# A decoder step's S5 seam: output gates and branch splits reordered, S5 output tiles computed in pairs

## The chip, the cores and the metric

One Trainium2 chip; the kernel runs on 1 of its cores. The metric is device microseconds (us) of one execution. Engines of the core, as the profile names them: PE (TensorE matmul), PEld (TensorE weight load, which overlaps PE), DVE (VectorE), ACT (ScalarE), POOL (GpSimd) and SP (SyncE, which here only issues DMAs).

## The reference, cut to what matters

One layer for 512 prompt tokens and 32 sample tokens (544 columns in all), model width 1024. An S5 branch (a diagonal state-space scan) and an HGRN2 branch (a gated linear recurrence) run side by side on one input projection and are merged by sigmoid gates; an MLP follows.

```python
h = rms_norm(x, norm_mix_pre)
proj = h @ w_in + b_in
u, q, f, i, g, gate_s5, gate_hg = jnp.split(proj, SPLIT_POINTS, axis=-1)
y_s5 = s5_mixer(u, ...)          # scan, gelu, then y * sigmoid(y @ w_glu + b_glu)
y_hg = hgrn2_mixer(q, f, i, g, ...)  # recurrence, norm, then o * silu(g)
merged = sigmoid(gate_s5) * (y_s5 @ w_br_s5) + sigmoid(gate_hg) * (y_hg @ w_br_hg)
x = x + rms_norm(merged @ w_out, norm_mix_post)
```

Further outputs are the new states of both branches.

## The kernel before, in words

**Products.** Every large product is computed in fp32r with operands split into a high part (`wh`, `xh`) and a low part (`wl`, `xl`): three matmuls per 128 x 128 block of weights, each for two halves of the 544 columns, so six matmuls per block (`dense`, L108 to L116). ACT casts the high part of a weight block (`S.copy(wh, wt)`, L99), DVE subtracts for the low part (L71). The same two-step cut of an activation is `split` (ACT L132, then DVE L71). `weights` (L83) loads one block by SP into one of 3 `wt` buffers and cuts it into one of 2 `wh` and 2 `wl` buffers. An output tile of `dense` lies in PSUM, in one of 2 `psd` buffers.

**Order of work.** The program's planner places each engine's instructions one after the other: among those that it holds ready, the one traced earliest goes first. `tc.high_priority(offset=n)` makes an instruction count as traced n instructions earlier; `WAHEAD` is 100 (weights), `EAHEAD` 50 (reading out a PSUM tile). `tc.manual_schedule(engines=...)` keeps the listed engines in the order written. The whole middle of the kernel (L1038 to L1063) is written by hand for PE alone.

**Fill queue.** In that middle, PE's small matmuls of the recurrences are interleaved with steps of the large products. A queue `fill.todo` holds generators, one per output tile; each step (`next`) is one block of 128 rows, six matmuls, and a tile has 8 steps. `fill.run(n)` takes n steps at a place in the code; the constants F1, F2, F3, FH, FY, FD (L480) are those n. The queue holds tiles of the HGRN2 inputs, then pairs of `hgrn_gate` tiles (silu(g), multiplied into `yhg`: ACT L522, DVE L74, DVE L71) and sigmoid gate tiles (`gate_tiles`, ACT L1016): 2 and 3, eight gate tiles, 4 and 5, eight gate tiles, 6 and 7; and last the eight `br_hg` tiles (yhg @ w_br_hg). When `s5_tables` starts, four steps of one of the first eight gate tiles, three more of them, and all behind them are left. `hgrn_gate` 6 and 7 are appended (L1057) after all gate tiles.

**S5 in the middle.** `s5_tables` (L834) computes tables on DVE (`ct`, `st`; `QR`, `QN` on SBUF of `Er`, `Ei`) and stores them to DRAM. `s5_late` (L922) runs for two halves of the groups, hf = 0 and 1: load `U`, `PT`, `Q`, `tab`; matmuls `psdS`; a scan on DVE; FH = 22 fill steps; `HB` from the scan (ACT L977); matmuls `psy` in four parts with FY = 3 steps between; FD = 12 steps after hf = 0; then the result goes to DRAM (`y_d`). `PT` and `HB` share memory, so `PT` and `U` of hf = 1 load after the last `psy` of hf = 0.

**HGRN2 branch.** The first step of `br_hg(0)` traces the cuts of its input (`split(*ys_[k], yhg[:, k])`, L1029). The tiles `yh`, `yl` use the memory of `hh`, `hl`, the projection's input, so a cut can run only when the last projection tile has read its block k.

**S5 output.** After the middle (L1069 on): `yt` comes back from DRAM, is cut to `zh`, `zl`; four tiles `ps_gl` (y @ w_glu), each followed by two sigmoids (L1093, L1095), the product `yn` on DVE and the cut to `sh`, `sl`; then eight tiles `ps_bs` (y_s5 @ w_br_s5), each followed by a product with the gate (which frees the PSUM buffer), a sum and a cut (`ms_`). Four weight blocks hold two tiles each. Here no engine's order is written by hand.

Of the kernel before, what the change touches and what calls it, by code (L numbers as in the profile page):

```python
# [9 lines left out]
F32 = mybir.dt.float32  # L10
# [35 lines left out]
def layer(ctx, tc, a, o):  # L46
# [23 lines left out]
    def tt(out, x, y, op, e=None):  # L70
        (e or V).tensor_tensor(out=out, in0=x, in1=y, op=op)  # L71
# [13 lines left out]
    def weights(src, name, res=None, ahead=WAHEAD):  # L85

        n = 1
        for d in src.shape[1:]:
            n *= d
        if len(src.shape) == 3:  # L90
            src = src.rearrange("p a b -> p (a b)")
        elif len(src.shape) == 4:
            src = src.rearrange("p a b c -> p (a b c)")
        with tc.high_priority(offset=ahead):
            wt = wp.tile([P, n], F32, tag="wt", name=f"wt_{name}", bufs=3)
            nc.sync.dma_start(out=wt, in_=src)
# [11 lines left out]
    def dense(ps, wh, wl, xs, first=True, last=True):  # L108

        n = len(xs)  # L110
        for k, (xh, xl) in enumerate(xs):
            c = slice(k * P, (k + 1) * P)
            f, l = first and k == 0, last and k == n - 1
            for w, x, st, sp in ((wh, xh, f, False), (wh, xl, False, False), (wl, xh, False, l)):
                for i in range(2):
                    mm(ps[:, i, 0:int(np.prod(x[i].shape[1:]))], lhsT=w[:, c], rhs=x[i], start=st, stop=sp)  # L116
# [11 lines left out]
    def dense_tile(name):  # L128
        return psd.tile([P, 2, 512], F32, tag="d", name=name)

    def split(hi, lo, src):
        S.copy(hi, src)  # L132
        tt(lo, src, hi.bitcast(F32), SUB)
# [343 lines left out]

    fill = Fill()

    F1, F2, F3, FL, FK, FO, FN, FH, FY, FD, FS = 44, 1, 32, 5, 4, 2, 3, 22, 3, 12, 2  # L480


    def hgrn_in(g, gp):
# [33 lines left out]
    def hgrn_gate(h, gp):  # L517
        m = 28 + h
        ps = yield from inproj(m)
        sg = gp.tile([P, 2, HT], F32, tag="sg", name=f"sg{m}")  # L520
        with tc.high_priority(offset=EAHEAD):
            S.activation(sg, ps[:, :, 0:HT], AF.Sigmoid, bias=b_in[:, m:m + 1])  # L522
            stt(sg, ps[:, :, 0:HT], b_in[:, m:m + 1], sg, ADD, MUL)
        y = yhg[:, h].rearrange("p (a b) -> p a b", a=2)
        tt(y, y, sg, MUL)
# [499 lines left out]
    def br_hg(m):  # L1025
        if m == 0:
            ys_ = pair_k("y")
            for k in range(8):
                split(*ys_[k], yhg[:, k])  # L1029
            yx.extend(views(ys_))  # L1030
        wh, wl = weights(a["w_br_hg"][m], f"bh{m}")
        ps = dense_tile(f"ps_bh{m}")
        yield from dense_steps(ps, wh, wl, yx)
        with tc.high_priority(offset=EAHEAD):
            gv = sgate[1][m].rearrange("p (a b) -> p a b", a=2)
            tt(gv, ps[:, :, 0:HT], gv, MUL)

    with tc.manual_schedule(engines={ET.PE}):  # L1038
        T = [hgrn_in(g, gp) for g in range(3)]
        s5a = ExitStack()  # L1040
        s5k = s5_parameters(s5a.enter_context(tc.tile_pool(name="s5a", bufs=1, reuse_waits="tile", side="right")))
        with tc.tile_pool(name="hcore", bufs=1, reuse_waits="tile", side="right") as hp:
            scT = [hp.tile([P, 2, NP_], F32, tag=f"scT{i}", name=f"scT{i}") for i in range(2)]
            scS = [hp.tile([NS, 2, NS], F32, tag=f"scS{i}", name=f"scS{i}") for i in range(2)]
            qm = hp.tile([P, 2, 8 * 36], F32, tag="qm", name="qm")
            for t in scT + scS + [qm]:
                G.memset(t, 0.0)
            for g in range(4):
                if g:
                    fill.add(hgrn_gate(2 * g - 2, gp), hgrn_gate(2 * g - 1, gp))  # L1050
                if g == 1:
                    T.append(hgrn_in(3, gp))
                elif g:
                    sgate[3 - g] = gate_tiles(3 - g)
                hgrn_core(g, T[g], hp, scT, scS, qm)
        s5a.close()
        fill.add(hgrn_gate(6, gp), hgrn_gate(7, gp))  # L1057
        with tc.tile_pool(name="s5p", bufs=1, reuse_waits="tile", side="right") as sp:
            s5_tables(sp, s5k)
        fill.add(*(br_hg(m) for m in range(8)))  # L1060
        fill.run(F3)
        with tc.tile_pool(name="s5", bufs=1, reuse_waits="tile") as sp:
            s5_late(sp, s5k)  # L1063
        fill.run()
# [4 lines left out]
    with tc.tile_pool(name="glu", bufs=1, reuse_waits="tile") as lp:  # L1069
        yt = lp.tile([P, 4, 576], F32, tag="yt", name="yt")  # L1070
        for k in range(4):
            nc.gpsimd.dma_start(out=yt[:, k].rearrange("p (t x) -> p t x", t=8),
                                in_=y_d.rearrange("t c g x -> c g t x")[4 * k:4 * k + 4]
                                .rearrange("c g t x -> (c g) t x"))
        zh = lp.tile([P, 4, 576], F32R, tag="zh", name="zh")
        zl = lp.tile([P, 4, 576], F32R, tag="zl", name="zl")
        for k in range(4):
            split(zh[:, k], zl[:, k], yt[:, k])
        sv = lambda z: [z[:, 0:288], z[:, 288:576].rearrange("p (t x) -> p t x", t=4)[:, :, 0:64]]
        zx = [(sv(zh[:, k]), sv(zl[:, k])) for k in range(4)]  # L1080
        b_glu = lp.tile([P, 4], F32, tag="b_glu", name="b_glu")
        nc.gpsimd.dma_start(out=b_glu, in_=a["b_glu"])
        sh = lp.tile([P, 4, NT], F32R, tag="sh", name="sh")
        sl = lp.tile([P, 4, NT], F32R, tag="sl", name="sl")
        for mc in range(2):
            wh, wl = weights(a["w_glu"][mc], f"gl{mc}")
            for i in range(2):
                m = 2 * mc + i
                ps = dense_tile(f"ps_gl{m}")
                dense(ps, wh[:, 512 * i:512 * i + 512], wl[:, 512 * i:512 * i + 512], zx)  # L1090
                with tc.high_priority(offset=EAHEAD):
                    sg = lp.tile([P, 8, 72], F32, tag="sgl", name=f"sgl{m}", bufs=2)
                    S.activation(sg[:, 0:4].rearrange("p t x -> p (t x)"), ps[:, 0, 0:288], AF.Sigmoid,  # L1093
                                 bias=b_glu[:, m:m + 1])
                    S.activation(sg[:, 4:8, 0:64], ps[:, 1, 0:256].rearrange("p (t x) -> p t x", t=4), AF.Sigmoid,  # L1095
                                 bias=b_glu[:, m:m + 1])
                    yn = lp.tile([P, 2, HT], F32, tag="yn", name=f"yn{m}", bufs=2)
                    yv = yt[:, m].rearrange("p (t x) -> p t x", t=8)
                    pv = lambda z: z[:, :, 0:64].rearrange("p t (h j) -> p h j t", h=2)
                    sv2 = lambda z: z[:, 0:4, 64:72].rearrange("p t (h j) -> p h j t", h=2)  # L1100
                    tt(yn[:, :, 0:256].rearrange("p h (j t) -> p h j t", t=8), pv(yv), pv(sg), MUL)
                    tt(yn[:, :, 256:HT].rearrange("p h (j t) -> p h j t", t=4), sv2(yv), sv2(sg), MUL)
                    split(sh[:, m], sl[:, m], yn.rearrange("p a b -> p (a b)"))
        sx = [(halves(sh[:, k]), halves(sl[:, k])) for k in range(4)]
        if "dbg_ys5" in o:
            nc.sync.dma_start(out=o["dbg_ys5"], in_=sh.bitcast(F32))
        for mc in range(4):
            wh, wl = weights(a["w_br_s5"][mc], f"bs{mc}")
            for i in range(2):
                m = 2 * mc + i  # L1110
                ps = dense_tile(f"ps_bs{m}")
                dense(ps, wh[:, 512 * i:512 * i + 512], wl[:, 512 * i:512 * i + 512], sx)
                with tc.high_priority(offset=EAHEAD):
                    gt = sgate[0][m]
                    gv = gt.rearrange("p (a b) -> p a b", a=2)
                    tt(gv, ps[:, :, 0:HT], gv, MUL)
                    tt(gt, gt, sgate[1][m], ADD)
                    split(*ms_[m], gt)
    hin.close()
    kept.close()  # L1120
    S.activation(scr1, ms_[7][0][:, 0:1], AF.Abs_reciprocal_sqrt, scale=0.0, bias=one_t)
# [597 lines left out]
```

## Time and profile before

| | us |
|---|---|
| three executions | 965.05, 965.63, 968.43 (median 965.63) |
| the profiled execution | 966.16 |
| its span, first to last instruction | 964.3 |
| PE busy | 943.5 (98%) |
| PEld busy | 919.8 (95%) |
| DVE busy | 621.8 (64%) |
| ACT busy | 446.2 (46%) |

All times in rows are from the start of the span. A row of a timeline gives start, duration, engine, line, operation, tiles, and in brackets how long the engine was idle before it and what ended that. Matmuls are pipelined: one that takes 0.29 us by its row is followed by the next after 0.127 us.

### The profile page before, as it was taken

To read this page: it belongs to the slowest core of one execution; us is meant where nothing else is said; L and a number is where in the kernel's file an instruction comes from. 1 tells how busy PE (TensorE), PEld (TensorE's weight loads), DVE (VectorE), ACT (ScalarE), POOL (GpSimd) and SP (SyncE) were. 2 spreads that over 40 slices of the span, in tenths; PEclk is the share of its full clock that TensorE was granted. 3 is DMA by queue.
4 is the path that set the end of the run, shared out by engine and by line. 5 is a ranking of instruction groups with operands and counts; after the bars stand their busy time and mean duration, and the time that the engine had idled before them with its cause. 6 is when DMAs were issued, how large, how long until landed. Compare 5 with 4: busy or idle time off the path is not lost.

```text
span 964.3 us, 21356 instructions
## 1 busy us (share of the span) xinstructions
PE 943.5 (98%) x9124; PEld 919.8 (95%) x9124; DVE 621.8 (64%) x1158; ACT 446.2 (46%) x835; POOL 62.6 (6%) x104
## 2 busy tenths in 40 slices
PE   8999999999999999999999999999999999999995
PEld 5999999989999999999999999999999999999994
DVE  6777669486693888558368558463673475447747
ACT  5744364544534523564243647343562265216623
POOL 2100000000000000422100000000100110010000
PEclk9999999999999999999999999999999999999998
DMA  7352242142423437666432514334544454356502
GB/s 251 98 147 67 67 135 71 50 155 67 149 68 91 140 125 249 223 193 205 131 91 88 175 45 158 110 109 122 133 151 102 107 155 131 103 125 167 180 2 92
DMA packets 45407, 121.26 MB, mean 126 GB/s; under 512 B 9121, under 2 KB 12577, under 8 KB 44673
## 3 DMA queue, kind: packets, MB, share of 16 engines
q1 hardware_dynamic: 37664, 97.20, 31.5%
q0 software_dynamic: 7360, 22.15, 8.8%
q8 instruction: 71, 1.16, 0.5%
q10 hardware_dynamic: 288, 0.56, 0.2%
q14 instruction: 24, 0.19, 0.1%
HBM read 101.66 MB, written 17.06 MB: 123 GB/s over the span
## 4 chain that ended last, share of the span: by engine, by line
PE 87%; DVE 6%; ACT 3%; DMA 2%; issue 2%; SPq 0%; DVEq 0%; ACTq 0%; POOLq 0%
PE ps_in L116 23%; PE ps_d L116 17%; PE ps_u L1324 8%; PE ps_u L126 7%; PE ps_bh L116 5%; PE ps_uy L1324 4%; PE ps_o L116 3%; PE ps_e L126 2%; PE ps_o L126 2%; PE ps_bs L116 2%; PE psL L643 2%; PE ps_uz L1324 2%; PE ps_u L116 1%; DMA tab<-tab_d 1%; PE psO L709 1%
## 5 line engine op out<-in xcount | busy, mean ns | idle before, releaser
L116 PE MATMUL ps_in<-hh,wh_in 128*128 128x272 f32 x736 | 159.0, 297 | 0.0
L116 PE MATMUL ps_in<-hl,wh_in 128*128 128x272 f32 x736 | 153.0, 289 | 0.0
L116 PE MATMUL ps_in<-hh,wl_in 128*128 128x272 f32 x736 | 152.3, 288 | 0.0
L116 PEld LDWEIGHTS ps_in<-hh,wh_in 128*128 128x128 f32 x736 | 115.3, 189 | 3.1 <-issue 1.8
L116 PEld LDWEIGHTS ps_in<-hl,wh_in 128*128 128x128 f32 x736 | 115.7, 189 | 0.0
L116 PEld LDWEIGHTS ps_in<-hh,wl_in 128*128 128x128 f32 x736 | 115.7, 188 | 0.0
L71 DVE TENSOR_TENSOR wl_in<-wt_in,wh_in 128x1024 fp32r<-128x1024 f32 (+1 forms) x54 | 61.7, 1144 | 61.1 <-ACT wh_in L99 58.5
L116 PE MATMUL ps_d<-a0l,wh_d 128*128 128x272 f32 x448 | 93.5, 290 | 0.0
L116 PE MATMUL ps_d<-a0h,wl_d 128*128 128x272 f32 x448 | 93.5, 290 | 0.0
L116 PE MATMUL ps_d<-a0h,wh_d 128*128 128x272 f32 x448 | 92.9, 289 | 0.4 <-DVE ov L71 0.4
L99 ACT CAST wh_in<-wt_in 128x1024 fp32r<-128x1024 f32 x46 | 48.3, 1052 | 91.3 <-PE ps_in L116 90.7
L116 PEld LDWEIGHTS ps_d<-a0h,wh_d 128*128 128x128 f32 x448 | 70.7, 188 | 0.6 <-PE ps_d L116 0.6
L116 PEld LDWEIGHTS ps_d<-a0h,wl_d 128*128 128x128 f32 x448 | 70.3, 188 | 0.9 <-DVE wl_d L71 0.6
L116 PEld LDWEIGHTS ps_d<-a0l,wh_d 128*128 128x128 f32 x448 | 70.6, 189 | 0.0
L71 DVE TENSOR_TENSOR ov<-ps_d,ov 128x544 f32<-128x544 f32 x24 | 17.4, 724 | 61.7 <-PE ps_d L116 61.7
L71 DVE TENSOR_TENSOR wl_d<-wt_d,wh_d 128x1024 fp32r<-128x1024 f32 x28 | 34.2, 1220 | 24.4 <-ACT wh_d L1277 18.9
L1277 ACT CAST wh_d<-wt_d 128x1024 fp32r<-128x1024 f32 x26 | 27.0, 1047 | 29.5 <-PE ps_d L116 18.1
L71 DVE TENSOR_TENSOR wl_S<-wt_S,wh_S 128x1024 fp32r<-128x1024 f32 x24 | 29.3, 1219 | 11.4 <-ACT wh_S L1277 11.4
L1277 ACT CAST wh_S<-wt_S 128x1024 fp32r<-128x1024 f32 x24 | 25.2, 1050 | 10.1 <-PE ps_d L116 10.1
L676 DVE COPY_PREDICATED scT<-masks,psL 32x128 f32<-32x128 uint8 x80 | 28.3, 354 | 2.3 <-PE psS L646 0.2
L116 PE MATMUL ps_bh<-yl,wh_bh 128*128 128x272 f32 x128 | 26.8, 291 | 1.4 <-DVE yl L71 1.4
L116 PE MATMUL ps_bh<-yh,wh_bh 128*128 128x272 f32 x128 | 27.1, 293 | 0.0
(552 smaller groups left out, 2312.5 us busy)
## 6 DMA issues: line engine op xcount, KB each, us to landing
wt_in<-in_w_in SPq DMA_DIRECT2D x52, 512.0 KB, 3.8
wt_d<-in_w_down SPq DMA_DIRECT2D x28, 512.0 KB, 3.9
wt_A<-in_w_up SPq DMA_DIRECT2D x12, 512.0 KB, 4.1
wt_S<-in_w_up SPq DMA_DIRECT2D x24, 256.0 KB, 2.7
wt_S<-in_w_up POOLq DMA_DIRECT2D x24, 256.0 KB, 4.6
s<-in_hg_s SPq DMA_DIRECT2D x8, 512.0 KB, 4.4
out_hg_s<-s SPq DMA_DIRECT2D x8, 512.0 KB, 3.6
wt_bh<-in_w_br_hg SPq DMA_DIRECT2D x8, 512.0 KB, 3.9
```

The lines of the kernel that those rows point to most:

```text
L71: (e or V).tensor_tensor(out=out, in0=x, in1=y, op=op)
L99: S.copy(wh, wt)
L116: mm(ps[:, i, 0:int(np.prod(x[i].shape[1:]))], lhsT=w[:, c], rhs=x[i], start=st, stop=sp)
L126: mm(ps[:, i, 0:HT], lhsT=ws[i][j][:, c], rhs=x[hf], start=st, stop=sp)
L643: mm(pq[sq * y:sq * y + m, 4 * i + w], lhsT=k[:, i, c:c + m], rhs=up(c, c + sq, i), start=True, stop=True)
L676: V.copy_predicated(blocks(sc[r], h)[:, :, y, :, 1], masks[r, L].rearrange("p x (n h) -> p x n h", h=h), pq[r].rearrange("p x (n h) -> p x ...
L709: mm(po[:, w], lhsT=sc[:, i, c], rhs=vt[:, i, w], start=True, stop=(w == 0))
L1277: S.copy(h, t)
L1324: mm(ps, lhsT=w[:, c], rhs=x_[:, k], start=(first and k == 0 and j == 0), stop=(k == 3 and j == 2), skip_group_check=True)
```

## The change

Five edits. FD goes from 12 to 9. The cuts of the HGRN2 branch's input are traced as if 400 instructions earlier. `hgrn_gate` 6 and 7 are put behind the tile in progress at the head of the fill queue, not at its end. ACT's order in the S5 output is written by hand: both `w_glu` blocks first, then the outputs of `ps_gl` 0 and 1, the first block of `w_br_s5`, the outputs of 2 and 3, the second block; in the `ps_bs` part the block after next comes ahead of the outputs of a pair. And `ps_bs` tiles 0 and 1 are computed together: blocks 0 to 2 of both, then block 3 of both; the outputs of every pair follow its two tiles.

```diff
-    F1, F2, F3, FL, FK, FO, FN, FH, FY, FD, FS = 44, 1, 32, 5, 4, 2, 3, 22, 3, 12, 2
+    F1, F2, F3, FL, FK, FO, FN, FH, FY, FD, FS = 44, 1, 32, 5, 4, 2, 3, 22, 3, 9, 2
@@ br_hg
-            for k in range(8):
-                split(*ys_[k], yhg[:, k])
+            with tc.high_priority(offset=400):
+                for k in range(8):
+                    split(*ys_[k], yhg[:, k])
@@ after the last hgrn_core
-        fill.add(hgrn_gate(6, gp), hgrn_gate(7, gp))
+        fill.todo[1:1] = [hgrn_gate(6, gp), hgrn_gate(7, gp)]
@@ S5 output; gl_out(m, ps) and bs_out(m, ps) hold the outputs' code as it was
-        for mc in range(2):
-            wh, wl = weights(a["w_glu"][mc], f"gl{mc}")
-            for i in range(2):
-                m = 2 * mc + i
-                ps = dense_tile(f"ps_gl{m}")
-                dense(ps, wh[:, 512 * i:512 * i + 512], wl[:, 512 * i:512 * i + 512], zx)
...
-        for mc in range(4):
-            wh, wl = weights(a["w_br_s5"][mc], f"bs{mc}")
-            for i in range(2):
-                m = 2 * mc + i
-                ps = dense_tile(f"ps_bs{m}")
-                dense(ps, wh[:, 512 * i:512 * i + 512], wl[:, 512 * i:512 * i + 512], sx)
...
+        wb = {}
+        with tc.manual_schedule(engines={ET.Activation}):
+            wg = [weights(a["w_glu"][mc], f"gl{mc}") for mc in range(2)]
+            for m in range(4):
+                c = slice(512 * (m % 2), 512 * (m % 2) + 512)
+                ps = dense_tile(f"ps_gl{m}")
+                dense(ps, wg[m // 2][0][:, c], wg[m // 2][1][:, c], zx)
+                gl_out(m, ps)
+                if m == 1:
+                    wb[0] = weights(a["w_br_s5"][0], "bs0")
+            wb[1] = weights(a["w_br_s5"][1], "bs1")
+            for mc in range(4):
+                wh, wl = wb[mc]
+                ps = [dense_tile(f"ps_bs{2 * mc + i}") for i in range(2)]
+                for ks in ((range(3), (3,)) if mc == 0 else (range(4),)):
+                    for i in range(2):
+                        for k in ks:
+                            c = slice(512 * i + k * P, 512 * i + k * P + P)
+                            dense(ps[i], wh[:, c], wl[:, c], sx[k:k + 1], first=(k == 0), last=(k == 3))
+                if mc < 2:
+                    wb[mc + 2] = weights(a["w_br_s5"][mc + 2], f"bs{mc + 2}")
+                for i in range(2):
+                    bs_out(2 * mc + i, ps[i])
```

## Rows read from the trace of the kernel before

**Rows 1.** PE's waits from 350 to 560: who, for whom, us, times, longest.

```profile
PE ps_bh L116 <- DVE yl L71: 1.4, 1, 1.4
PE ps_bs L116 <- ACT sh L132: 0.9, 1, 0.9
PE psy L990 <- ACT HB L977: 0.5, 1, 0.5
PE ps_bs L116 <- ACT sgl L1095: 0.2, 1, 0.2
```

**Rows 2.** Busy time by stretch: the stretch, its length, each engine, clock, DMA share, GB/s.

```profile
core 0: us, PE busy (x) PEld busy (x) DVE busy (x) ACT busy (x) POOL busy (x), PEclk, DMA share, GB/s
350.00:550.00 200.00, 197.08 (x1701) 195.18 (x1700) 133.85 (x205) 90.84 (x139) 29.45 (x44) 1.00 0.52 168
```

**Rows 3.** Chain of waits, a stretch of unbroken product: start, us, what.

```profile
468.06 22.84 PE ps_bh L116 x180
```

**Rows 4.** Timeline of PE, 429.8 to 436.9, where `br_hg` begins.

```profile
430.17 0.51 PE L116 MATMUL ps_bh<-yh,wh_bh 128*128 128x272 f32 x2
...
432.07 0.52 PE L116 MATMUL ps_bh<-yl,wh_bh 128*128 128x272 f32 x2 [1.39 <-DVE yl L71]
...
434.27 2.44 PE L949 MATMUL psdS<-U,PT 128*64 128x80 f32 x64
```

**Rows 5.** Timeline of ACT, 423 to 437.

```profile
423.86 3.82 ACT L980 COPY Tg<-T 128x2048 f32<-128x2048 f32 x1
...
428.20 1.04 ACT L99 CAST wh_bh<-wt_bh 128x1024 fp32r<-128x1024 f32 x1
429.14 0.44 ACT L1000 ACTIVATE gsq<-gsq 128x288 f32<-128x288 f32 x1
429.48 3.37 ACT L132 CAST yh<-yhg 128x544 fp32r<-128x544 f32 x6
```

**Rows 6.** Tile U, 420 to 436: its load's issue, and the load's time to landing.

```profile
L930 POOL DMA_DIRECT2D U<-u_d x1: 537/537/537, 424.1 to 424.1; - x1
...
DMA to landing us min/median/max: 6.2/6.2/6.2
```

**Rows 7.** Timeline of DVE, 345 to 386, in `s5_tables`.

```profile
349.39 0.78 DVE L74 SCALAR_TENSOR_TENSOR sg<-ps_in,b_in,sg 128x544 f32<-128x544 f32 x1
...
350.82 0.71 DVE L71 TENSOR_TENSOR yhg<-yhg,sg 128x544 f32<-128x544 f32 x1
...
366.62 1.23 DVE L71 TENSOR_TENSOR wl_in<-wt_in,wh_in 128x1024 fp32r<-128x1024 f32 x1 [3.25 <-ACT wh_in L99]
...
382.41 1.23 DVE L71 TENSOR_TENSOR QN<-QN,t 128x1024 f32<-128x1024 f32 x1
```

**Rows 8.** Timeline of ACT, 364 to 412, through hf = 0 of `s5_late`.

```profile
366.49 0.72 ACT L1016 ACTIVATE gate_q<-ps_in,b_in 128x544 f32<-128x544 f32 x1
...
390.74 0.62 ACT L940 COPY rh<-ex 128x512 f32<-128x512 f32 x1 [6.16 <-DMA q_d<-QN]
...
403.99 3.82 ACT L980 COPY Tg<-T 128x2048 f32<-128x2048 f32 x1
...
407.82 1.23 ACT L977 COPY HB<-di 64x504 f32<-64x504 f32 x2
```

**Rows 9.** Timeline of PE, 407.9 to 409.8.

```profile
409.19 0.48 PE L990 MATMUL psy<-HB,Q 128*128 128x144 f32 x2 [0.48 <-ACT HB L977]
```

**Rows 10.** Tile ps_bs: matmuls, ns min/median/max, first and last start.

```profile
L116 PE MATMUL ps_bs<-sh,wh_bs x64: 286/288/393, 502.8 to 527.9; 128*128 128x272 f32 x64
```

**Rows 11.** Timeline of ACT, 490 to 516.

```profile
503.60 1.04 ACT L99 CAST wh_bs<-wt_bs 128x1024 fp32r<-128x1024 f32 x1
504.55 0.50 ACT L1093 ACTIVATE sgl<-ps_gl,b_glu 128x288 f32<-128x288 f32 x1
```

**Rows 12.** Timeline of DVE, 500 to 520.

```profile
501.67 1.34 DVE L71 TENSOR_TENSOR yn<-yt,sgl 128x32 f32<-128x32 f32 x2
...
504.68 1.23 DVE L71 TENSOR_TENSOR wl_bs<-wt_bs,wh_bs 128x1024 fp32r<-128x1024 f32 x1 [0.23 <-ACT wh_bs L99]
...
509.42 0.72 DVE L71 TENSOR_TENSOR gate_q<-ps_bs,gate_q 128x544 f32<-128x544 f32 x1 [0.86 <-PE ps_bs L116]
```

More of the change, by code (lines that the diff above doesn't have):

```diff
@@ L1084, in layer @@
         sl = lp.tile([P, 4, NT], F32R, tag="sl", name="sl")
-        for mc in range(2):
-            wh, wl = weights(a["w_glu"][mc], f"gl{mc}")
-            for i in range(2):
-                m = 2 * mc + i
-                ps = dense_tile(f"ps_gl{m}")
-                dense(ps, wh[:, 512 * i:512 * i + 512], wl[:, 512 * i:512 * i + 512], zx)
[L1091 to L1103, printed above, removed]
@@ new lines, in gl_out @@
+        def gl_out(m, ps):
+            with tc.high_priority(offset=EAHEAD):
+                sg = lp.tile([P, 8, 72], F32, tag="sgl", name=f"sgl{m}", bufs=2)
+                S.activation(sg[:, 0:4].rearrange("p t x -> p (t x)"), ps[:, 0, 0:288], AF.Sigmoid,
+                             bias=b_glu[:, m:m + 1])
+                S.activation(sg[:, 4:8, 0:64], ps[:, 1, 0:256].rearrange("p (t x) -> p t x", t=4), AF.Sigmoid,
+                             bias=b_glu[:, m:m + 1])
+                yn = lp.tile([P, 2, HT], F32, tag="yn", name=f"yn{m}", bufs=2)
+                yv = yt[:, m].rearrange("p (t x) -> p t x", t=8)
+                pv = lambda z: z[:, :, 0:64].rearrange("p t (h j) -> p h j t", h=2)
+                sv2 = lambda z: z[:, 0:4, 64:72].rearrange("p t (h j) -> p h j t", h=2)
+                tt(yn[:, :, 0:256].rearrange("p h (j t) -> p h j t", t=8), pv(yv), pv(sg), MUL)
+                tt(yn[:, :, 256:HT].rearrange("p h (j t) -> p h j t", t=4), sv2(yv), sv2(sg), MUL)
+                split(sh[:, m], sl[:, m], yn.rearrange("p a b -> p (a b)"))
@@ L1106, in layer, with bs_out @@
             nc.sync.dma_start(out=o["dbg_ys5"], in_=sh.bitcast(F32))
-        for mc in range(4):
-            wh, wl = weights(a["w_br_s5"][mc], f"bs{mc}")
-            for i in range(2):
-                m = 2 * mc + i
-                ps = dense_tile(f"ps_bs{m}")
-                dense(ps, wh[:, 512 * i:512 * i + 512], wl[:, 512 * i:512 * i + 512], sx)
[L1113 to L1118, printed above, removed]
+        def bs_out(m, ps):
+            with tc.high_priority(offset=EAHEAD):
+                gt = sgate[0][m]
+                gv = gt.rearrange("p (a b) -> p a b", a=2)
+                tt(gv, ps[:, :, 0:HT], gv, MUL)
+                tt(gt, gt, sgate[1][m], ADD)
+                split(*ms_[m], gt)
+        wb = {}
[21 more added lines that the diff above has]
+                    bs_out(2 * mc + i, ps[i])
     hin.close()
```

## The prediction

> **What bounds the kernel now.** First PE's list of waits over the stretch that the edits touch, 350 to 560: it has only four entries, and they are the whole room there is [rows 1]. The stretch's busy times say the same: of 200 us PE idles 2.92 between 350 and 550 at full clock [rows 2]. An idle entry understates the loss, since a matmul's row outlasts its successor's start: 180 matmuls took 22.84 us, 0.127 us each [rows 3], so after the two at 430.17 the next was due at 430.42 and came at 432.07, a loss of 1.65 where the row shows 1.39 idle [rows 4]. I add this 0.26 to every entry: the start of `br_hg` 1.65; `psy` of hf = 0 waiting for `HB` 0.74; `ps_bs` waiting for a PSUM buffer that a sigmoid reads 0.45, and for `sh` 1.12. Together 3.96 us, 0.41% of the time. As PE is the path, each number below is time on it, or it is hidden.
>
> The Trainium skill (Trainium Kernel Development and Optimization, Best Practices) would have the distance judged by how busy the weight loads are, not the matmuls. Their row leaves 4.82 us idle in the stretch where the matmuls' leaves 2.92 [rows 2]; by that rule the ceiling of a gain is 4.8 and not 4.0.
>
> **Part 1: what fills PE around the `br_hg` seam (FD, gates, cuts).** The number of steps is the same, so PE's own work is. After `psy` of hf = 0, the queue before has nine projection steps left and then three of `br_hg(0)`; these three start at 430.17 and stall. With FD = 9 the `psdS` matmuls of hf = 1 come exactly at 430.17, and `br_hg(0)` behind them. The 1.65 goes. What is late next:
>
> (a) `psdS` needs `U`, which loads after `psy`: issued at 424.1, landing 6.2 us later, at 430.3 [rows 6]. PE is there at 430.2, and with the restart loses some 0.25. FD takes away the cover of three steps (2.3 us) that this load had; a load 1 us later costs 1 us more.
>
> (b) `psdS` lasts 2.4 (row start 434.27, 64 matmuls, 2.44) [rows 4], so `br_hg(0)` is due at about 432.9. Cuts now outrank weight casts (400 against 100). They can't run early: `yh` lies in `hh`'s memory, block 0 of which the last projection tile, eight steps of 0.76 that end at 430.17, first gives up at 424.9. At that time ACT is in the copy of `Tg`, 423.86 to 427.68 [rows 5]. Before, it took the weights' cast first (428.20) and the cuts after it (429.48, six in 3.37, 0.56 each) [rows 5]. Now the cuts come first as far as they are ready. Seven of them (3.9), one gate output (0.72, [rows 8]), the sigmoid (0.44) and the cast itself (1.04) end at 427.7 + 6.1 = 433.8: PE waits 0.9, and half a microsecond of matmuls later another 0.7 for DVE's low half (1.23 by the like operation of [rows 12]). That is 1.6. Lower end 0, if the cast keeps its place. Upper end 2.9, if the eighth cut and the second gate output (0.56 + 0.72) go ahead as well. I take 1.6, since the new order is just what the offsets say and the rows give every duration of it. If the cast is early instead, the cuts' low halves hold DVE and the scan of hf = 1, whose `HB` now falls due three steps earlier, is the next thing late; I put that inside the same ends.
>
> Seam: -1.65 + 0.25 + 1.6 = +0.2 (ends -1.4 and +1.5).
>
> (c) The gates moved up. Each costs ACT 0.72 and DVE 0.78 + 0.71 [rows 7, 8]. They leave DVE at the seam, where PE no longer waits for them. But gates 4 and 5 are pushed back by two tiles: from 349 on DVE [rows 7] to the tile whose output ACT takes at 366.49 [rows 8] and the one after it. There DVE works on the `QR`/`QN` products, which end at 382.41 + 1.23 = 383.64 [rows 7]. All that follows hangs on that end: the store of `QN`, for which ACT waits until 390.74 (6.16 idle), then the scan, then the copies to `HB` at 407.82 [rows 8], for which PE waits at 409.19 [rows 9]. This chain has no slack; it is 0.74 late already. So DVE work put into it counts in full: 0 at the lower end (hidden in the hole of 3.25 before 366.62 [rows 7]; the new work comes after that hole, so only a rearrangement would do it), 2 x 1.49 = 3.0 at the upper. The first gate's product (0.78) is traced within 50 instructions of the chain and outranks it; the other three operations rank behind it and run only where the chain pauses. At 350.82 such a second product did slip into the table chain [rows 7], which speaks for more. I take +0.8. Gates 6 and 7 add the same 3.0 about 16 steps after the tables begin, well ahead of the hole of 3.25 at 366.62 [rows 7], which takes it up; without it they would cost 3.0 by the same chain.
>
> **Part 2: the S5 output.** PE enters `ps_bs` at 502.8 [rows 10]. Before, ACT cast weights at 503.60 (1.04) ahead of the fourth sigmoid pair at 504.55 [rows 11]. By hand the cast follows, so the sigmoids can start 0.5 to 1.0 earlier: the first `w_br_s5` cast now comes after the outputs of `ps_gl` 1 and pushes tile 2's by up to 1.04, which takes back half; I take 0.5. That frees the PSUM buffer before PE asks for it (505.1): -0.45. With blocks 0 to 2 of both tiles first, 36 matmuls last until 502.8 + 4.6 = 507.4, and `sh` of the fourth tile is then due half a microsecond later than before and comes half a microsecond earlier: -1.12. If one of the two fails, its 0.45 or 1.12 stays.
>
> What it adds: tiles 0 and 1 now end six matmuls apart, at 508.2 and 508.9, and tile 2 needs tile 0's buffer at once. DVE has the product that frees it (0.72 [rows 12]) and the low half of the second block (1.23 [rows 12]), both due in the same microsecond: cast of that block after the last `sh`, low half until about 509.1, product until 509.8, PE waits 0.9 + 0.26, say 1.1. Lower end 0.1 (the product alone), upper 2.5, if the first block's low half, now cast after `ps_gl` 1, also lies behind a `yn` pair (1.34, [rows 12]). ACT's waits in its new order hold only cuts of `ms_`, and those are read after the last `ps_bs` tile, which begins its last block at 527.9 [rows 10]. SP issues the same loads in the same order, into the same three buffers.
>
> Seam: -1.57 + 1.1 = -0.45 (ends -1.5 and +0.9).
>
> **Sum.** +0.2 + 0.8 - 0.45 = +0.55 us. The profiled execution took 966.16 (span 964.3 and 1.86 around it); it would be 966.7. The median shown is 0.53 lower, 965.63: forecast 966.2 us, no change that can be measured. What a measurement of this kernel tells from none is about 0.5%, 4.8 us; the three runs alone lie 3.4 apart.
>
> **Rivals.**
>
> *All four waits go.* The cast keeps its place, the chain of `QN` gets shorter by what left it, the S5 output is clean: -3.96 + 0.25 + 0.1 = -3.6, 962.0. For it: every wait has an edit aimed at it or near it. Against: ACT has 3.8 of `Tg` and some 4.5 of cuts in the 9 us before `br_hg`, and no edit touches the `QN` chain but to add to it.
>
> *Slower: the whole DVE work of gates 4 and 5 lands in the `QN` chain.* Place: DVE, 367 to 384; price 3.0 at `psy` of hf = 0, in place of my 0.8; it decides from the first tenth of a microsecond by which `QN` ends after 383.64. 965.63 + 0.2 - 0.45 + 3.0 = 968.4. For it: the precedent at 350.82. Against: ACT idles 6.16 before 390.74 for the store alone [rows 8], and work that now interrupts the scan behind it could move into that wait.
>
> *The offset does nothing*, because memory and `Tg` hold the cuts anyway and PE waits as long at the new place as at the old: the S5 output alone counts, 965.2.
>
> *A gain up to the weight loads' ceiling*, 4.8: 960.8. Nothing in PE's own list of waits supports the further 0.9.
>
> **How the numbers follow.** Forecast 0.43, its own range 964.5 to 967.5; slower through `QN` 0.29; all waits gone 0.20; offset idle 0.05; weight-load ceiling 0.03. The range takes in both sides: 962.0 at the bottom (the second of these), at the top the upper ends of `br_hg` and `QN` together with the S5 term, 965.63 + 1.5 + 3.0 - 0.45 = 969.7. Faster by over 0.5% means below 960.8, more than all waits hold: 0.03. Slower by over 0.5% means over 970.5, all upper ends at once (+5.4): 0.06. Within: 0.91.
>
> **What would show it.** In PE's waits after: no entry at `ps_bh` for `yl`; a short one at `psdS` for `U`; one at `ps_bh` for `wh_bh` (step b; if it is absent and ACT's cast precedes the cuts, b was wrong). The last `QN` on DVE later than 383.6, and the entry of `psy` for `HB` longer than 0.5 by as much (c). In the S5 output no entry for `sh` or the sigmoid, and one at `ps_bs` for the gate's product on DVE. The prediction fails if PE's idle between 350 and 560 falls below 1.5 us or rises over 6.

## The result, and the profile after

The changed kernel takes 971.53 us (median of 10 runs, 969.30 to 974.14), the kernel before in the same comparison 965.94 (10 runs, 965.05 to 969.93): ratio 1.0052, 95% interval 1.0041 to 1.0064. It is slower, by 5.6 us. Forecast were 966.2 and a range of 962.0 to 969.7.

The profiled execution of the changed kernel took 974.14 us (span 972.3), 8.0 more than the profiled one of before. It is the slowest of the ten executions and shows the lowest mean granted clock of them (0.991; the other nine 0.992 to 0.996), so stretches are read from it with care. To see where the time went, PE's timeline is cut at five first starts: the last `psN` (before anything that was edited), `psFq` (the end of the stretch in which DVE computes the S5 tables), `psy` of hf = 0, `ps_gl`, `ps_o`. The stretch from `psy` to `ps_gl` is called the seam below; the wait for `HB` of hf = 0 lies in it, since the first matmuls of `psy` read parts of `HB` that are ready earlier.

| us | psN to psFq | to psy | to ps_gl | to ps_o | after |
|---|---|---|---|---|---|
| before | 34.18 | 54.77 | 82.42 | 37.83 | 435.70 |
| changed | 39.74 | 55.67 | 84.06 | 36.99 | 435.69 |
| difference | +5.56 | +0.90 | +1.64 | -0.84 | 0 |

The missing 0.76 lies ahead of the last `psN` (319.36 and 320.12); in twelve other profiles that start lies anywhere from 318.5 to 322.4, so it belongs to no edit.

PE's waits in the changed kernel, 320 to 560 (who, for whom, us, times, longest), are the answer to [rows 1]:

```profile
PE ps_in L116 <- DVE t L71: 2.5, 1, 2.5
PE ps_in L116 <- DVE wl_in L71: 1.1, 1, 1.1
PE ps_bh L116 <- ACT wh_bh L99: 0.8, 1, 0.8
PE ps_in L116 <- DVE sg L74: 0.7, 1, 0.7
PE psdS L949 <- DVE ysb L71: 0.6, 1, 0.6
PE ps_bh L116 <- DVE wl_bh L71: 0.5, 1, 0.5
PE ps_bs L116 <- DVE gate_q L71: 0.3, 1, 0.3
PE psdS L949 <- DMA U<-u_d: 0.2, 1, 0.2
```

All four waits of before are gone; eight others stand there. The largest two lie in 325 to 346, where the kernel before had none. From 350 to 560, the stretch that the prediction called the whole room, PE idles 3.13 us after and idled 2.92 before, so the sign written down for failure (over 6) did not show: the loss lies ahead of that window. The row after:

```profile
350.00:560.00 210.00, 206.87 (x1765) 204.97 (x1764) 133.65 (x201) 92.99 (x142) 29.42 (x44) 0.99 0.49 164
```

The busy row of the kernel before for 325 to 345, which I had not read (columns as in [rows 2]):

```profile
325.00:345.00 20.00, 20.00 (x160) 20.00 (x160) 19.96 (x45) 6.61 (x10) 1.60 (x4) 1.00 0.43 125
```

DVE is busy for 19.96 of 20 us there, and PE for all of them. The same row after:

```profile
325.00:345.00 20.00, 16.71 (x130) 16.27 (x129) 20.00 (x45) 6.59 (x10) 1.60 (x4) 1.00 0.34 99
```

DVE's timeline of the changed kernel in that stretch shows what the two gates did to its queue:

```profile
330.53 0.78 DVE L74 SCALAR_TENSOR_TENSOR sg<-ps_in,b_in,sg 128x544 f32<-128x544 f32 x1
...
335.68 1.22 DVE L71 TENSOR_TENSOR wl_in<-wt_in,wh_in 128x1024 fp32r<-128x1024 f32 x1
336.81 1.22 DVE L71 TENSOR_TENSOR t<-Ei,a2i 128x1024 f32<-128x1024 f32 x1
...
341.70 1.22 DVE L71 TENSOR_TENSOR wl_in<-wt_in,wh_in 128x1024 fp32r<-128x1024 f32 x1
...
344.37 0.78 DVE L74 SCALAR_TENSOR_TENSOR sg<-ps_in,b_in,sg 128x544 f32<-128x544 f32 x1
```

and ACT's shows when their inputs were there:

```profile
329.95 1.04 ACT L99 CAST wh_in<-wt_in 128x1024 fp32r<-128x1024 f32 x1
335.16 1.05 ACT L99 CAST wh_in<-wt_in 128x1024 fp32r<-128x1024 f32 x1 [4.17 <-PE ps_in L116]
336.11 0.71 ACT L522 ACTIVATE sg<-ps_in,b_in 128x544 f32<-128x544 f32 x1
```

The cast at 329.95 ends at 331.0, its low half starts 4.7 later, at 335.68; the cast at 335.16 ends at 336.2, its low half starts 5.5 later, at 341.70. The second gate's sigmoid ends at 336.8, and the product that reads the same PSUM tile, and so frees it, starts 7.5 later, at 344.37. In the kernel before DVE's queue had the low half of the cast that ended at 335.45 at once:

```profile
335.48 1.23 DVE L71 TENSOR_TENSOR wl_in<-wt_in,wh_in 128x1024 fp32r<-128x1024 f32 x1
```

So a full DVE does not by itself delay the low halves: before, it was as full, and they came at once. What changed is their place in its queue. Behind the first gate's product (330.53, 0.78), DVE does nothing but table operations from 331.22 to 335.68, and the low half comes after them.

What stood at this place before were sigmoid tiles, which ACT alone reads out of PSUM; a `hgrn_gate` tile hands its buffer to DVE. PE's timeline has both ends of it:

```profile
336.96 0.52 PE L116 MATMUL ps_in<-hh,wl_in 128*128 128x272 f32 x2 [1.08 <-DVE wl_in L71]
...
345.30 0.49 PE L116 MATMUL ps_in<-hh,wh_in 128*128 128x272 f32 x2 [2.52 <-DVE t L71]
...
346.91 0.65 PE L116 MATMUL ps_in<-hh,wh_in 128*128 128x272 f32 x2
```

Start to start the two waits cost 1.23 and 2.68 over the usual 0.127. The low half that was 5.5 late ended at 342.92, while PE stood waiting for the buffer, so it added no wait of its own. The releaser of the second is named `t`, since it ended last; the product at 344.37, which ends just before PE starts, is the one that reads the buffer. And from 346.9 to 350.1 the matmuls start 0.227 apart: 15 times 0.1 is 1.5, nearly all that remains of 5.56. The granted clock of 340 to 350 is 0.84, so part of it ran at the lower level, 1.2 GHz:

```profile
340.00:350.00 10.00, 7.48 (x49) 7.29 (x48) 10.00 (x26) 1.66 (x2) 0.00 (x0) 0.84 0.25 74
```

At the seam, ACT's timeline answers to [rows 5]; the cast of `wh_bh` now comes after all eight cuts:

```profile
430.47 3.82 ACT L980 COPY Tg<-T 128x2048 f32<-128x2048 f32 x1
434.20 1.74 ACT L132 CAST yh<-yhg 128x544 fp32r<-128x544 f32 x3
435.84 0.71 ACT L1016 ACTIVATE gate_v<-ps_in,b_in 128x544 f32<-128x544 f32 x1
436.45 1.73 ACT L132 CAST yh<-yhg 128x544 fp32r<-128x544 f32 x3
438.08 0.44 ACT L1000 ACTIVATE gsq<-gsq 128x288 f32<-128x288 f32 x1
438.43 1.18 ACT L132 CAST yh<-yhg 128x544 fp32r<-128x544 f32 x2
439.51 0.71 ACT L1016 ACTIVATE gate_v<-ps_in,b_in 128x544 f32<-128x544 f32 x1
440.12 1.03 ACT L99 CAST wh_bh<-wt_bh 128x1024 fp32r<-128x1024 f32 x1
```

and PE's answers to [rows 4]:

```profile
437.10 1.88 PE L949 MATMUL psdS<-U,PT 128*64 128x80 f32 x48 [0.19 <-DMA U<-u_d]
439.63 0.78 PE L949 MATMUL psdS<-U,PT 128*64 128x80 f32 x16 [0.65 <-DVE ysb L71]
441.21 0.52 PE L116 MATMUL ps_bh<-yh,wh_bh 128*128 128x272 f32 x2 [0.80 <-ACT wh_bh L99]
...
442.46 0.82 PE L116 MATMUL ps_bh<-yh,wl_bh 128*128 128x272 f32 x2 [0.49 <-DVE wl_bh L71]
```

### The profile page after: what moved, and what is told of

The parts are those of the page before. It is cut to its first block, busy times and chain, and to the rows that moved or that the text cites. A ratio compares the mean times of both kernels' runs of the same rounds, so it can differ in the third digit from the quotient of the medians.

```text
span 972.3 us, 21361 instructions
## 1 busy us (share of the span) xinstructions
PE 947.6 (97%) x9124; PEld 923.8 (95%) x9124; DVE 621.2 (64%) x1158; ACT 445.9 (46%) x835; POOL 62.5 (6%) x104
## 4 chain that ended last, share of the span: by engine, by line
PE 89%; DVE 6%; ACT 3%; issue 1%; DMA 1%; SPq 0%; DVEq 0%; ACTq 0%
PE ps_in L116 24%; PE ps_d L116 17%; PE ps_u L1344 7%; PE ps_u L126 7%; PE ps_bh L116 5%; PE ps_uy L1344 4%; PE ps_o L116 2%; PE ps_bs L116 2%; PE ps_e L126 2%; PE ps_o L126 2%; PE psL L643 2%; PE ps_uz L1344 2%; PE ps_gl L116 1%; PE ps_u L116 1%; DVE t L71 1%
## 5 line engine op out<-in xcount | busy, mean ns | idle before, releaser
L116 PE MATMUL ps_bh<-yh,wl_bh 128*128 128x272 f32 x128 | 27.4, 296 | 0.5 <-DVE wl_bh L71 0.5
```

## The experiments

Theory A, after the result: gates 6 and 7 are the loss, because they put DVE work into the stretch where DVE has no free time. Rivals: the PSUM buffer, held until DVE reads it, and not DVE's time; the place in PE's own order; FD = 9 and the offset, not the gates. Each kernel is compared with the kernel before in its own runs on the same chip (median 966.71, 968.33 and 966.35 in the three groups of four), so ratios are what to compare. All compute the whole layer.

**One part undone, one part alone**

`e1_gates_last`, the changed kernel with the gates at the end of the queue again:

```diff
-        fill.todo[1:1] = [hgrn_gate(6, gp), hgrn_gate(7, gp)]
+        fill.add(hgrn_gate(6, gp), hgrn_gate(7, gp))
```

> The changed kernel with hgrn_gate 6 and 7 back at the end of the fill queue, all else as changed. Theory A: the loss is the two gate tiles run while DVE computes the S5 tables: in the profile after, PE waits there for wl_in (1.1 idle) and for sg (2.5 idle), runs some 15 matmuls at 0.227 us instead of 0.127 behind it, and waits 0.7 more for the next gate pair; 5.6 + 1.0 us in all by the same points of both timelines. Then this one takes 965 to 967 us (ratio to before 0.999 to 1.001). Rival B: the loss is at the br_hg seam (offset 400 and FD = 9), where the profile after shows 0.2, 0.6, 0.8 and 0.5 idle: then it stays at 970 or more (ratio over 1.004).

968.33 us, ratio 1.0015 (1.0002 to 1.0027). The tables' stretch is back at 34.18 to the hundredth. The rest is 84.86 from `psy` to `ps_gl` (2.44 more than before) and -0.86 in the S5 output. The ratio lies above the range of A (up to 1.001) and below that of B (from 1.004): some two thirds of the loss are the gates' place, and what is left is the seam.

`e2_gates_alone`, the kernel before with that line alone:

```diff
-        fill.add(hgrn_gate(6, gp), hgrn_gate(7, gp))
+        fill.todo[1:1] = [hgrn_gate(6, gp), hgrn_gate(7, gp)]
```

> The kernel before with only hgrn_gate 6 and 7 moved up. Theory A: it carries the whole loss, 5 to 7 us, less what the br_hg seam wins back when the gates have left it (at most 1.7): 969 to 972 us (ratio 1.003 to 1.007), with the wait for sg at ps_in near 342. Rival B: 965 to 966.5.

970.91, ratio 1.0041 (1.0026 to 1.0055). Tables 38.24, with the same two waits, 1.1 and 2.5; the stretch to `psy` +0.77; the seam 82.13, 0.3 better than before (its wait for `yl` shrinks from 1.4 to 0.9, and the one for `HB` grows from 0.5 to 0.9). One edit of a line makes most of the loss. Here the matmuls behind the 2.5 stay 0.127 apart, and the row of 340 to 350 has the clock at 1.00 beside the same busy time of PE as above:

```profile
340.00:350.00 10.00, 7.48 (x60) 7.29 (x59) 10.00 (x24) 1.66 (x2) 0.00 (x0) 1.00 0.26 76
```

`e3_s5out_alone`, the kernel before with the S5 output of the changed one (both functions, ACT's order by hand, tiles 0 and 1 together); against the changed one:

```diff
-    ... = 44, 1, 32, 5, 4, 2, 3, 22, 3, 9, 2
+    ... = 44, 1, 32, 5, 4, 2, 3, 22, 3, 12, 2
-            with tc.high_priority(offset=400):
-        fill.todo[1:1] = [hgrn_gate(6, gp), hgrn_gate(7, gp)]
+        fill.add(hgrn_gate(6, gp), hgrn_gate(7, gp))
```

> The kernel before with only the S5 output as changed (ACT's order by hand, tiles in pairs). From the two profiles the stretch from ps_gl to ps_o became 0.85 us shorter: waits of 0.2 and 0.9 idle gone, one of 0.3 for the gate's product new. Theory A and rival B both say 964.8 to 965.4 (ratio 0.999); the prediction's term of -0.45 says 965.5.

965.97, ratio 0.9990 (0.9979 to 1.0001). The S5 output is 36.99 in place of 37.83, with one wait left, 0.3 for `gate_q`. It does what it says; 0.84 of 966 is at the edge of what these runs can tell. The stretches ahead, which this kernel does not edit, are 55.04 and 82.99 in its trace against 54.77 and 82.42 in the kernel before, so between two single traces a difference of up to 0.6 there says little.

**Why the gates stall PE**

`e4_act_frees`: ACT copies the gate's product out of PSUM at once, DVE multiplies from there.

```diff
-            stt(sg, ps[:, :, 0:HT], b_in[:, m:m + 1], sg, ADD, MUL)
+            gx = gp.tile([P, 2, HT], F32, tag="gx", name=f"gx{m}", bufs=1)
+            S.activation(gx, ps[:, :, 0:HT], AF.Identity, bias=b_in[:, m:m + 1])
+        tt(sg, gx, sg, MUL)
```

(for gates 6 and 7 alone)

> The changed kernel, but for gates 6 and 7 ACT copies the projection out of PSUM (Identity with bias, 0.7 us more on ACT each) and DVE multiplies from SBUF; DVE has as much work, but no longer frees the PSUM buffer. Theory A1 (PE waits because the PSUM buffer is freed by a DVE queue that is full): the 2.5 wait for sg and the slow matmuls behind it go, about 4 us: 966.5 to 968.5. Theory A2 (it is DVE's load itself, which delays the weights' low halves): unchanged within 1 us of the changed kernel, 970.5 to 972.

975.36, ratio 1.0081 (1.0065 to 1.0097); tables 40.74. By the ratios that is 0.3% worse than the changed kernel, which neither theory had. So the PSUM buffer alone is not it: with PSUM free (ACT's second copy ends at 338.4, although it waited 1.22 for DVE to give back the one `gx` buffer), PE runs on into the next thing that waits in the same queue, a weight block's low half, and waits 4.2 in one piece. The cast of that block ended at 335.87, and its low half starts 8.7 later. PE's and DVE's timelines:

```profile
345.85 0.82 PE L116 MATMUL ps_in<-hh,wl_in 128*128 128x272 f32 x2 [4.23 <-DVE wl_in L71]
```

```profile
342.41 0.71 DVE L71 TENSOR_TENSOR yhg<-yhg,sg 128x544 f32<-128x544 f32 x1
343.05 1.21 DVE L71 TENSOR_TENSOR Ei<-Ei,t 128x1024 f32<-128x1024 f32 x1
...
344.59 1.21 DVE L71 TENSOR_TENSOR wl_in<-wt_in,wh_in 128x1024 fp32r<-128x1024 f32 x1
```

`e5_gates_pool`: as e4, and both multiplications of gates 6 and 7 on POOL.

```diff
+        e = V if h < 6 else G
+            tt(sg, gx, sg, MUL, e)
-        tt(y, y, sg, MUL)
+        tt(y, y, sg, MUL, e)
```

> The changed kernel with gates 6 and 7 taken off DVE: ACT reads the product out of PSUM (Identity with the bias, one copy more per gate on ACT), and both multiplications run on POOL. Theory A (DVE's queue is full from 324 to 345 and every operation put into it there pushes the low halves of the weights back by its own length): the stretch from the last psN to psFq goes from 39.7 back to 34.2 to 35.5 us, PE's waits for DVE there vanish, and the time is 966 to 968.5. Theory B (it is the place of the two tiles in PE's own order, with the sigmoid and copy on ACT and the tiles' weights, and not DVE's products): the stretch stays at 38 or more and the time at 970 or more. A result between, 36 to 38, would say that POOL's use of the memory port or ACT's copy costs as well.

971.17, ratio 1.0037 (1.0024 to 1.0051). The tables' stretch is back at 34.76, as A had it, with PE's order and ACT's work as in e4: the loss there comes from the two products in DVE's queue, not from the place of the tiles in PE's order. Whether it is the time that they take on DVE, or the order in which the planner then puts the low halves among the table operations, is not separated. The total is not what A said. The loss moved on: the stretch to `psy` is 58.94, 4.2 over before, with a wait of 2.45 for the product of gate 5, which stands in DVE's queue among the `QR`/`QN` products, and 14 matmuls 0.227 apart behind it. The chain on DVE is not shorter than before: `QN` ends 68.01 after the last `psN`, in place of 64.28, and four DVE operations beside POOL's products took 3.8 longer together (last section).

`t_mid`: the gates behind the first tiles of the other kind, ten places into the queue.

```diff
-        fill.todo[1:1] = [hgrn_gate(6, gp), hgrn_gate(7, gp)]
+        fill.todo[9:9] = [hgrn_gate(6, gp), hgrn_gate(7, gp)]
```

> The changed kernel with gates 6 and 7 put ten places into the queue of what fills PE instead of two, behind the first tiles of the other gate, so that their products fall due on DVE between 384 and 390, where DVE waits for the store of QN. Theory A (it is where the products meet DVE that decides): the tables' stretch is back at 34.2 to 34.8, the wait for HB does not come back as it did with the gates at the end, and the time is 966 to 968. Theory B (the products cost 1.5 us each wherever they stand ahead of the seam, through the chain of QN): 969 or more, with a wait for HB or for psFq's inputs in the list of PE.

968.04, ratio 1.0006 (0.9993 to 1.0020). Tables 34.18; the products run at 387.16 and 395.83, the first in DVE's wait for the store of `QN`, the second in the scan behind it, and PE's wait for `HB` is 1.0. The other half of A was too rosy: that wait did come back, and the stretch to `psy` is 55.89, 1.1 over before, with a new wait of 0.49 for a low half.

**The seam: FD and the offset**

`e8_cast_first`, the changed kernel with the first `br_hg` weights cast ahead of the cuts:

```diff
-        wh, wl = weights(a["w_br_hg"][m], f"bh{m}")
+        wh, wl = weights(a["w_br_hg"][m], f"bh{m}", ahead=WAHEAD if m else 600)
```

> The changed kernel with one distance altered: the weights of the first br_hg tile are cast ahead of the cuts on ACT (their priority offset 600 instead of the common 100). Theory A (step b of the prediction: the cuts that outrank the cast cost PE 0.8 for the high half and 0.5 for the low half, and the half clock behind): no wait for wh_bh and wl_bh of tile 0, the seam 1.3 to 2.5 us shorter, 969.0 to 970.3 against 971.5 of the changed kernel. Theory B (the same work is late in another order: the cuts now come later and PE waits for yh or yl as it did in the kernel before): a wait for yh or yl of 1 to 1.7 us in its place, and the time stays at 971 to 972.

974.36, ratio 1.0064 (1.0041 to 1.0088); seam 84.78, 0.7 longer than in the changed kernel. The waits for `wh_bh` and `wl_bh` are gone and another stands in their place, of neither tile that I named: `dS`, which ACT copies out of PSUM behind all eight cuts and two gate outputs.

```profile
441.76 1.07 PE L949 MATMUL psdS<-U,PT 128*64 128x80 f32 x16 [2.50 <-ACT dS L951]
```

`e6_fd12`, the changed kernel with FD = 12 again:

```diff
-    ... = 44, 1, 32, 5, 4, 2, 3, 22, 3, 9, 2
+    ... = 44, 1, 32, 5, 4, 2, 3, 22, 3, 12, 2
```

> The changed kernel with FD back at 12, so that psdS of the second half comes behind the first br_hg tile as before; gates 6 and 7 stay moved up, the cuts stay split off. Theory A (the tables' stretch is the loss, FD itself is worth little): that stretch stays near 39.7, the waits for U and ysb vanish, one for yl or wh_bh of 1 to 2 us stays at the seam, 971 to 972.5. Theory B (FD = 9 moves the half clock and the short waits into the seam and costs 1 to 2 us by itself): 969 to 970.5, the seam shorter by as much.

974.42, ratio 1.0066 (1.0046 to 1.0086); seam 84.87. A had the tables' stretch (39.73) and the waits for `U` and `ysb` gone; the wait that came is in neither theory. With the offset but without `psdS` in front, PE is at `br_hg` sooner, and a gate output that frees its PSUM buffer stands on ACT behind the cuts:

```profile
440.36 0.52 PE L116 MATMUL ps_bh<-yh,wh_bh 128*128 128x272 f32 x2 [3.37 <-ACT gate_v L1016]
```

So FD = 9 is worth 0.8 at the seam beside the offset, by these two traces; the intervals of the two ratios overlap. Whether it is a gain without the offset, three kernels tried:

```diff
-            with tc.high_priority(offset=400):
-                for k in range(8):
-                    split(*ys_[k], yhg[:, k])
+            for k in range(8):
+                split(*ys_[k], yhg[:, k])
```

`e7_no_offset` is the changed kernel with this edit alone, `e9_fd9_no_offset` has the gates last besides, `t_mid_no_offset` has them ten places in.

> The changed kernel with the priority offset of 400 taken off the cuts; FD = 9, the gates moved up and the S5 output stay. Theory A (the offset is what fills the seam: 84.1 us from psy of the first half to ps_gl against 82.4 in the kernel before and 82.1 in the kernel with the gates alone): that stretch is 82 to 83, no wait for wh_bh and wl_bh, and the time 969 to 970.5 against 971.5 of the changed kernel, since the tables' 39.7 stays. Theory B (ACT is full from Tg to the dS copies, and whatever order its work has there, PE waits for what comes last; with the cast ahead of the cuts it was dS, 2.5): the stretch stays at 83.5 to 85, with a wait for yl or dS of 1.5 to 2.5, and the time at 971 to 972.5.

> The kernel before with FD = 9 and the changed S5 output alone: no gates moved up, no offset on the cuts. Tables at 34.2. Theory A (FD = 9 by itself fills the hole at the first br_hg tile): psy to ps_gl 81.5 to 82.4, ratio to the kernel before 0.997 to 0.999. Theory B (psdS of the second half moved ahead finds its inputs late, U and ysb, and ACT's queue as full as before): 83 to 84.9, as in the kernel with the gates last (84.9), ratio 1.000 to 1.002.

> The changed kernel without the offset, and with gates 6 and 7 ten places into the queue. Against the kernel with those gates and the offset (ratio 1.0006, tables 34.2, psFq to psy 55.9, psy to ps_gl 84.0): Theory A (the offset costs 1.6): psy to ps_gl 82 to 82.8, the wait for HB of 1.0 stays, ratio 0.998 to 0.9995. Theory B (ACT's total work binds at the seam): 83.5 to 85, ratio 1.000 to 1.0015.

978.58, 975.21 and 974.68: ratios 1.0124 (1.0107 to 1.0141), 1.0087 (1.0072 to 1.0102) and 1.0084 (1.0067 to 1.0101). The seam is 89.54, 92.42 and 90.58. Both theories fell in all three, by 4.5 to 7.5 us over the upper end of B: I had looked at ACT, and the wait is on DVE. PE's waits of e9 from 430 to 452:

```profile
PE ps_bh L116 <- DVE yl L71: 7.2, 2, 4.0
PE psdS L949 <- DMA U<-u_d: 0.3, 1, 0.3
```

and DVE's timeline of e9:

```profile
439.05 0.68 DVE L71 TENSOR_TENSOR dr<-dr,t 128x512 f32<-128x512 f32 x1
439.65 0.72 DVE L71 TENSOR_TENSOR yl<-yhg,yh 128x544 fp32r<-128x544 f32 x1
440.29 0.68 DVE L71 TENSOR_TENSOR t<-dS,tab 128x512 f32<-128x512 f32 x1
440.89 0.72 DVE L71 TENSOR_TENSOR yl<-yhg,yh 128x544 fp32r<-128x544 f32 x1
...
446.77 0.72 DVE L71 TENSOR_TENSOR yl<-yhg,yh 128x544 fp32r<-128x544 f32 x1
```

With `psdS` ahead of `br_hg(0)`, the scan of hf = 1 is ready before the last cuts, it was traced earlier, and so the low halves `yl` stand among its operations. The offset is what puts the cuts ahead of that scan. FD = 9 and the offset are one edit: by itself the offset costs 2.7 us at this place and FD = 9 costs 7 to 10, in single traces and with the matmuls at the lower clock behind the stops.

`e10_mid_fd12`, the kernel of e3 with the gates ten places in:

```diff
-        fill.add(hgrn_gate(6, gp), hgrn_gate(7, gp))
+        fill.todo[9:9] = [hgrn_gate(6, gp), hgrn_gate(7, gp)]
```

> The kernel before with the changed S5 output and the gates ten places into the queue; FD = 12 and no offset, as before. It prices the new place alone. Theory A (the products meet DVE in the scan behind the store of QN and cost the HB wait 0.5 more, and give back up to 0.7 at the seam, where two gates less stand): tables 34.2, psFq to psy 55.3 to 55.9, psy to ps_gl 81.5 to 82.4, ratio 0.998 to 0.9995. Theory B (moving gates anywhere ahead only delays the other gates and gains nothing at the seam): psy to ps_gl 82.8 or more, ratio 1.000 to 1.001.

966.46, ratio 0.9997 (0.9983 to 1.0010): tables 34.18, to `psy` 55.79, seam 82.29, S5 output 37.00. The new place gives 0.1 to 0.7 at the seam (82.42 in the kernel before, 82.99 in e3). It takes 0.75 to 1.0 ahead of `psy`, where PE now waits 0.49 for a low half `wl_in`; the wait for `HB` is 1.04, as in e3 (1.02).

The seam (`psy` to `ps_gl`) of all kernels but e8, by the two settings:

| us | FD 12, no offset | FD 12, offset | FD 9, no offset | FD 9, offset |
|---|---|---|---|---|
| gates early | 82.13 | 84.87 | 89.54 | 84.06; e4 82.79, e5 82.77 |
| gates ten places in | 82.29 | | 90.58 | 84.02 |
| gates last | 82.42, 82.99 | | 92.42 | 84.86 |

The kernels e4 and e5 have the same four waits at the seam as the changed one, each to within 0.1 us, but no matmuls at the lower clock behind them. The rows of 435 to 450 of the changed kernel and of e4 show the same busy time of PE, at two clocks:

```profile
435.00:450.00 15.00, 12.87 (x132) 12.17 (x131) 14.20 (x22) 9.71 (x21) 4.96 (x6) 0.89 0.80 292
```

```profile
435.00:450.00 15.00, 12.87 (x143) 12.17 (x142) 13.32 (x21) 11.18 (x23) 4.96 (x6) 1.00 0.78 294
```

So with the gates early the pair as changed costs 0.7 over neither at full clock and 1.9 with the stretch at the lower one. The 0.7 is flattered by the wait for `HB`, 0.9 in e2 and absent in e4. Ten places in, with that wait in both kernels and the clock at full, the pair costs 1.7; with the gates last, 1.9 to 2.4. No kernel beats the one before by more than the runs can tell; the best is e3, which beats the changed one by 0.6%.

## Why the prediction was wrong

**The step that failed** is the last sentence of (c): "Gates 6 and 7 add the same 3.0 about 16 steps after the tables begin, well ahead of the hole of 3.25 at 366.62 [rows 7], which takes it up; without it they would cost 3.0 by the same chain." The amount of DVE work, 3.0, is right. The hole takes up a delay of the `QN` chain that has come through to 366, and that chain was all I asked about. I had taken 350 to 560 as the stretch that the edits touch, and the two tiles land ahead of it: their sigmoids run at 329 and 336. Between 325 and 345 the same queue also makes what PE needs within one tile (6.1 us): the low halves, and the release of the gates' own PSUM buffers. Where the products went into it, these came 4.7, 5.5 and 7.5 late, and PE paid 3.9 in two waits and 1.5 more at the lower clock: 5.56 in the profiled execution (4.06 in e2, without the lower clock) for a term costed at nothing. Shown by e1 and e2 (the one line, out and in), by e4 (not the buffer alone) and e5 (not PE's order). The delays are longer than the products ahead of them, and before, an equally full DVE made the low halves at once; why the planner placed them behind the table operations is not tested, and stays open.

The rival "Slower", with DVE work in the `QN` chain, had the engine and the sign, but the wrong gates, place and price. `QN` ends 31.50 after the first `psFq` (391.36 less 359.86), before 30.10: 1.4 later, of my 0.8 to 3.0. One of its products is plain in DVE's timeline, a gate's second product between the last `QN` operations:

```profile
389.51 0.71 DVE L71 TENSOR_TENSOR yhg<-yhg,sg 128x544 f32<-128x544 f32 x1
390.15 1.21 DVE L71 TENSOR_TENSOR QN<-QN,t 128x1024 f32<-128x1024 f32 x1
```

Yet the wait for `HB` [rows 9] did not grow by 0.8: it is gone. PE was held 0.86 ahead of it, by the product of gate 5 (0.7 idle), and from `rh` to the last `HB` ACT and DVE took 16.2 (398.22 to 414.44) in place of 17.1 [rows 8], where the kernel before had a weight cast and a gate output (1.05 and 0.71) between `rh` and `dS`. So (c) came out at 0.90 - 0.64 = +0.3 for +0.8: inside its ends, by a way that I had not seen, which is luck. In e2, the gates alone, the wait for `HB` did grow, by 0.42 behind a stretch 0.77 longer: 1.2 together.

**Seam.** -1.65 came as said, and (a): 0.35 for 0.25. (b), the cast behind the cuts: 0.91 and 0.65 start to start over 0.127, together 1.56 for 1.6. That agreement is luck. The order on ACT is the one written down for the upper end, all eight cuts and both gate outputs ahead of the cast, at a price of 2.9; two things took it down: `psdS` itself was held by `ysb`, which hid 0.75, and ACT needed 6.9 from the end of `Tg` to the end of the cast (434.29 to 441.15) where the rows summed to 7.4. Not in the sum: `psdS` waiting 0.75 for `ysb`, which DVE makes and which ends the use of a `psy` buffer, and 14 matmuls behind the stop at the lower clock, 1.6. Start to start, 4.3 came (0.35, 1.56, 0.75, 1.6) and 2.7 went (1.55 for `yl`, 0.64 for `HB`, some 0.5 in gaps of 0.1 each): +1.6, as in the table. At full clock (e4 and e5) the table's difference is +0.4, and +1.0 when the 0.64 of `HB`, which the prediction has under (c), is put aside. Of the 0.8 over the forecast of +0.2, `ysb` is 0.75. e8 shows what I had taken as the lower end of (b), "if the cast keeps its place", to be no gain at all.

**S5 output.** -0.84 for -0.45: the two waits went (1.58 start to start), and `gate_q` came with the blocks at the pair's end, together 0.74 where I took 1.1.

**The bounds.** The upper ends summed to +5.4 only because gates 6 and 7 had none but zero. By the working's own words, 3.0 "without it", the range would have reached 972.7 and held the result, though by the `QN` chain and not by what came. The other rivals came to nothing: wherever one of the four waits went, others came into its room; the offset, taken off beside FD = 9, is worth 5.5 us at the seam (e7); and no kernel came near the weight loads' ceiling.

Of the profile's 8.0 the median shows 5.6. The waits at full clock sum to 4.5 (4.06 as in e2, 0.90, 0.4 as in e4, less 0.84), the stretches at the lower clock to some 2.8 (39.74 less 38.24 of e2, 84.06 less 82.79 of e4), the start to 0.76. How many executions have these stretches isn't known, since only one of each kernel has a trace; that the profiled one has the lowest clock of the ten fits with its having more of them than most.

## What to carry to other kernels

Before a step is moved to another place, read the busy row of every engine that it uses at the place where it lands, in a window as long as PE's prefetch (here one tile, 6 us), and ask what else in that engine's queue PE needs within that time; a free stretch 20 us later is no cover. If the busy share there is near 1, the moved work is not free. Its length, here 3.0, is a first estimate and no upper end: what PE waits for can be put behind more than the moved work itself (here 3.9), and the lower clock behind the stop can come on top. Two edits that order the same queue, as FD and the offset here, have to be priced together: with the gates early, their four combinations ranged over 7 us at the seam, and neither alone was better than none.

## What the runs showed of the hardware

After a stop of PE the lower clock comes sometimes and not always. With the same wait of 2.5 us, in the same place, the changed kernel, e6 and e8 ran some 15 matmuls 0.227 apart afterwards (granted clock 0.83 or 0.84 in 340 to 350) and e2 and e7 none (1.00). e4, after 4.2, had it at once (0.69). At the seam, the same four waits of 0.2 to 0.8 were followed by 14 matmuls at the lower clock in the changed kernel (0.89 in 435 to 450) and by none in e4 and e5 (1.00). What decides isn't settled.

POOL's products slowed DVE's. In e5 the products of 128 x 544 on POOL took 1.36 to 2.22 us, and DVE's operations beside them were longer: one of 128 x 512, 0.69 in the kernel before, took 1.84, one of 128 x 32, 0.19 before, 1.35. Both ended within 0.6 us after the POOL product that ran beside them (334.49 and 333.94; 340.67 and 340.62). The Trainium skill (Trainium Architecture — The Big Picture, What this means for kernel authors) says that the port pair that DVE and GpSimd share is an exclusive lock, not a split of bandwidth; these rows agree. DVE's timeline of e5, and POOL's:

```profile
332.65 1.84 DVE L71 TENSOR_TENSOR t<-Ei,a1i 128x512 f32<-128x512 f32 x1
...
339.32 1.35 DVE L71 TENSOR_TENSOR ct<-ct,t 128x32 f32<-128x32 f32 x1
```

```profile
331.72 2.22 POOL L71 TENSOR_TENSOR yhg<-yhg,sg 128x544 f32<-128x544 f32 x1
...
338.93 1.69 POOL L71 TENSOR_TENSOR yhg<-yhg,sg 128x544 f32<-128x544 f32 x1
```
